# Weights times v by query halves: 1536 columns a unit for 2048, v's halves copied by its loads, and the filler's low parts on GpSimd

## The chip, the core and the metric

The kernel runs on one core of a Trainium2 chip. The metric is the device time of one execution in microseconds (us). A core has TensorE (PE, which multiplies matrices; PEld is its weight load), VectorE (DVE), ScalarE (ACT), GpSimd (POOL), and SyncE (SP), which here only issues DMAs. POOL issues some DMAs too; the queue of each of the two is in order.

## The reference

One block of a decoder, for 1024 tokens of 1024 channels: a modulated rmsnorm, one wide projection, two branches (sliding-window attention with sinks, and a linear recurrence), each gated and projected, merged by sigmoid gates, one output projection, a residual and a last rmsnorm. The change touches the attention alone:

```python
# 16 query heads in 4 groups (one k and v for 4 heads), head size 64, blocks of 128 queries
s = einsum('bnqkgd,bnskd->bnkgqs', qb, kb) / sqrt(64)   # 128 queries, 256 keys: own and last block
diff = qi + 128 - kj
band = (diff >= 0) & (diff < 128)                       # each query sees exactly 128 keys
m = maximum(max(s), sink)
p = exp(s - m);  denom = sum(p) + exp(sink - m)
o = einsum('bnkgqs,bnskd->bnqkgd', p / denom, vb)
```

A query q of block n sees the keys up to q of its own block and the keys behind q of the block before: for each of the 128 key positions exactly one of two. All is float32 in and out. Where the kernel multiplies in a shorter format it splits a number into a high and a low part (names in h and l: `phc`, `plc` for the weights, `wh`, `wl` for a projection's weights), and v's row holds both parts side by side, 64 columns each.

## The kernel before

The work is one long program, whose order on every engine is written out by hand up to the end of the attention. Behind that a list scheduler orders the tail.

Ahead of the attention come the modulation and the wide projection (`bk`, L709). Then follow 32 attention units, u = 0 to 31, eight query blocks n for each of the four groups, four heads in a unit. Between the steps of the units stand pieces of other matmuls, the filler: first the last of the projection, then the projection of the recurrent branch (`rp`, L173), which reads `yh` and `yl` (or, for the first two of eight rows, `hha` and `hla`) loaded from DRAM by SP, and weights `wh`, `wl`. Behind the attention come the projection of its output (`pmain`), the merge and the output projection.

A pass u of the loop does, on PE: the scores of unit u (`scores`, L1330, into the two banks of `s_ps`, which exist once), a piece of the filler (12 matmuls of 512 columns), the four transposes of unit u-2 (`transposed`, L1369, into `pt`), and the weights times v of unit u-3 (`values`, L1403, into `pv`). On ACT: the copy of the scores out of PSUM (L1339), the exponentials of unit u-1 (L1355), the high part `phc` of unit u-2 (L1374), half of the join of unit u-3 (L1412, L1413), a cast of filler weights (L105). On DVE: the scores of the last block where the mask asks for them (COPY_PREDICATED, L1345), the maximum (L1350), the low parts of the filler's weights (`rest`, L111), the division (L1362), the low part `plc` (L1380), the rest of the join (L1423, L1424), and the gating of finished pairs of units (L1538, L1548). On POOL: the sinks of unit u+1 (L1318), the masked copies `phm` and `plm` of unit u-2 (L1389), loads of v and some stores.

Since each key position stands for one key of two, only one transposed matrix of weights is kept for 128 positions, and the product is made as "all positions times the block before" plus "the masked positions times the difference of the two blocks". So a unit needs four matmuls: `phc` and `plc` with v of the block before, `phm` and `plm` with the difference. At n = 0 there is no block before, and two matmuls do. v of each group is prepared earlier (`v_prep`, L1154): `vs` is v in its two parts, `dv` the difference, and both are stored to `vd_d`, v shifted by one block. `load_v` (L1305) loads for two units at once, on POOL's queue, with two buffers.

The filler's weights go through `prep_r`: the cast is put on one list, the rest on another. The rests are issued on DVE in the next pass, ahead of the filler, and the casts on ACT at a pass's end. SP's queue takes the loads of keys, queries, gates, filler weights and of `yh`, `yl`.

In SBUF the tiles of attention are laid over tiles of the projection that are used no more. The first instruction that writes such a tile waits for the last that reads the old one. Among the old ones are the tiles from which `yh_d` and `yl_d` are stored, on POOL's queue, just ahead of the attention.

Of the kernel before, what the change touches and what calls it, by code (L numbers as in the profile page):

```python
# [12 lines left out]
F32 = mybir.dt.float32  # L13
# [5 lines left out]
ALU = mybir.AluOpType  # L19
# [31 lines left out]
BANKS = (0, 1, 2, 3), (4, 5, 6, 7)  # L51


@with_exitstack
def tile_hybrid_block(ctx, tc, x, pk, rows, posr, posi, c_row, w_ss, w_gate, w_main, w_v,
# [53 lines left out]
    def rest(dst, src, scale=1.0):  # L109
        if scale == 1.0:  # L110
            V.tensor_tensor(out=dst[1][:], in0=src, in1=f32(dst[0][:]), op=ALU.subtract)  # L111
# [18 lines left out]
    vd_d = [tc.dram_tile([P, 8, 2, P], F32, name=f"vd_d{g}") for g in range(NG)]  # L130
# [1023 lines left out]
    def v_prep(g):  # L1154
# [19 lines left out]
        def f3():  # L1174
# [3 lines left out]
            dma(vd_d[g][:, 1:8, 1, :], t["vs"][:, 0:7, :], G)  # L1178
            dma(vd_d[g][:, :, 0, :], t["dv"][:], G)
# [102 lines left out]
    def open_attn():  # L1282
# [9 lines left out]
        load_v(0)  # L1292

# [71 lines left out]
    def transposed(u):  # L1365
        px = U.pop(("s", u))[1]
        pt = psx.tile([P, 4, P], F32, tag="t", name="pt")
        for j in range(4):
            W["pe"] = T.transpose(pt[:, j, :], px[:, j, 0:P], ident[:])  # L1369
        U["t", u] = [pt]  # L1370

    def split_a(u):
        phc = at.tile([P, 4, P], F32R, tag="phc", name="phc")
        A.copy(phc[:], U["t", u][0][:])  # L1374
        U["t", u].append(phc)

    def split_d(u):
        pt, phc = U.pop(("t", u))
        plc = at.tile([P, 4, P], F32R, tag="plc", name="plc")
        V.tensor_tensor(out=plc[:], in0=pt[:], in1=f32(phc[:]), op=ALU.subtract)  # L1380
        U["m", u] = phc, plc

    def masks(u):
        phc, plc = U["m", u]
        ms = []
        if u % 8:
            for s_, tag in ((phc, "phm"), (plc, "plm")):
                d_ = W["yo"].tile([P, 4, P], F32R, tag=tag, name=tag)
                G.affine_select(out=d_[:], in_=f32(s_[:]), pattern=[[0, 4], [1, P]],  # L1389
                                compare_op=ALU.is_ge, fill=0.0, base=0,  # L1390
                                channel_multiplier=-1)
# [668 lines left out]
```

## Time and profile before

| | us |
|---|---|
| median of 3 runs | 907.04 (906.72 to 907.05) |
| the profiled execution | 907.17 |
| its span in the profile | 905.5 |
| PE busy | 895.4 (99%) |
| DVE busy | 717.1 (79%) |
| ACT busy | 567.4 (63%) |
| POOL busy | 124.7 (14%) |
| PE's granted clock | 0.999 |

All rows of the profile come from the profiled execution, whose time is its span and 1.67 us around it. The attention lies between 557.6 and 730.1 us of the span. A chain of waits is read from the end of the program back: at each step it goes to what released an instruction, or to the one before it on its engine. A row of a group of instructions gives line, engine, operation, what is written from what, the count, and then busy time and the mean of one in ns; behind the last bar stands the idle time of the engine ahead of it, and what ended it. A row of a stretch gives start and end, its length, the busy time of each engine with its count, PE's clock, the mean busy share of 16 DMA engines, and GB/s.

### The profile page before, as it was taken

What the parts mean: (1) busy time and instruction counts of PE and PEld (TensorE: products, weight loads), DVE (VectorE), ACT (ScalarE), POOL (GpSimd) and SP (SyncE); (2) the same over time, 40 slices, a digit from 0 to 9 for tenths busy, and PEclk for the clock granted to TensorE, in tenths of its full rate; (3) what the DMA queues carried; (4) which work ended last, traced back from release to release, by engine and by line L of the source; (5) the groups of instructions that cost most, each with busy time, mean ns of one, the idle gap of its engine ahead of it and who ended that gap; (6) DMA issues with size and microseconds to landing.
All of it is one profiled execution on the core that took longest, in us unless ns stands there. A gap on an engine that the chain in (4) does not pass through costs nothing.

```text
span 905.5 us, 12654 instructions
## 1 busy us (share of the span) xinstructions
PE 895.4 (99%) x4258; PEld 746.2 (82%) x4259; DVE 717.1 (79%) x1073; ACT 567.4 (63%) x1098; POOL 124.7 (14%) x216
## 2 busy tenths in 40 slices
PE   9999999999999999999999999999999999999997
PEld 6789888888888888888888888888888888888886
DVE  6987688988669875987788597999989846578855
ACT  7965554654566855786485884888888732115535
POOL 6520251200000000000000002343443300000000
PEclk9999999999999999999999999999999999999999
DMA  9829489772435353354446367996655289416604
GB/s 355 339 69 286 164 258 319 256 235 95 151 128 180 123 209 135 125 183 162 157 144 213 105 201 242 344 401 217 214 202 203 83 306 367 140 47 232 209 1 186
DMA packets 87349, 180.74 MB, mean 200 GB/s; under 512 B 8642, under 2 KB 29138, under 8 KB 87284
## 3 DMA queue, kind: packets, MB, share of 16 engines
q1 hardware_dynamic: 83200, 167.07, 52.5%
q0 software_dynamic: 3936, 12.59, 4.4%
q8 instruction: 34, 0.56, 0.3%
q14 instruction: 31, 0.25, 0.1%
q10 hardware_dynamic: 148, 0.27, 0.1%
HBM read 121.34 MB, written 58.95 MB: 199 GB/s over the span
## 4 chain that ended last, share of the span: by engine, by line
PE 52%; issue 42%; DVE 3%; ACT 2%; DMA 1%; POOL 0%; DVEq 0%; ACTq 0%; POOLq 0%
PE rp L173 14%; PE bk L709 10%; PE out L1863 6%; PE pmain L173 5%; PE s_ps L1330 3%; PE pv L1403 3%; PE pmain L485 2%; PE bk L485 2%; PE pt L1369 1%; DMA yl_d<-it 1%; PE pmain L1579 1%; PE pmain L1580 1%; PE pmain L1578 1%; ACT jk L1881 1%; PE bk L256 1%
## 5 line engine op out<-in xcount | busy, mean ns | idle before, releaser
L709 PE MATMUL bk<-nh,wh 128*128 128x512 f32 x368 | 143.4, 390 | 0.0
L709 PE MATMUL bk<-nl,wh 128*128 128x512 f32 x368 | 143.3, 389 | 0.0
L709 PE MATMUL bk<-nh,wl 128*128 128x512 f32 x368 | 98.4, 389 | 0.0
L111 DVE TENSOR_TENSOR wl<-r,wh 128x512 fp32r<-128x512 f32 x109 | 74.8, 692 | 23.3 <-ACT wh L105 23.2
L105 ACT CAST wh<-r 128x512 fp32r<-128x512 f32 x107 | 65.6, 618 | 32.1 <-PE rp L173 11.8
L709 PEld LDWEIGHTS bk<-nh,wl 128*128 128x128 f32 x368 | 69.1, 188 | 14.3
L709 PEld LDWEIGHTS bk<-nh,wh 128*128 128x128 f32 x368 | 69.2, 188 | 14.2
L709 PEld LDWEIGHTS bk<-nl,wh 128*128 128x128 f32 x368 | 69.1, 188 | 14.1
L709 PE MATMUL bk<-hh,wh 128*128 128x512 f32 x184 | 71.7, 390 | 0.0
L709 PE MATMUL bk<-hl,wh 128*128 128x512 f32 x184 | 71.6, 389 | 0.0
L111 DVE TENSOR_TENSOR wl<-ws,wh 128x512 fp32r<-128x512 f32 x76 | 52.1, 686 | 7.2 <-ACT wh L105 7.1
L62 POOL DMA_DIRECT2D yh_d<-av x1 | 0.6, 567 | 371.9 <-ACT av L1092 371.9
L1355 ACT ACTIVATE p<-p,small 128x129 f32<-128x129 f32 x128 | 50.0, 396 | 0.0
L709 PE MATMUL bk<-hh,wl 128*128 128x512 f32 x184 | 49.2, 389 | 0.0
L105 ACT CAST wh<-ws 128x512 fp32r<-128x512 f32 x76 | 46.0, 614 | 4.8 <-DVE ws L731 2.4
L709 PEld LDWEIGHTS bk<-hh,wl 128*128 128x128 f32 x184 | 34.6, 188 | 7.1
L709 PEld LDWEIGHTS bk<-hh,wh 128*128 128x128 f32 x184 | 34.6, 188 | 7.1
L709 PEld LDWEIGHTS bk<-hl,wh 128*128 128x128 f32 x184 | 34.6, 188 | 7.1
L1330 PEld LDWEIGHTS s_ps<-ks,qs 128*128 128x128 f32 x256 | 34.1, 189 | 4.4 <-DVE p L1345 2.0
L1330 PE MATMUL s_ps<-ks,qs 128*128 128x256 f32 (+1 forms) x256 | 35.6, 282 | 0.3 <-DVE p L1345 0.2
L709 PE MATMUL bk<-hha,wh 128*128 128x512 f32 x92 | 35.8, 390 | 0.0
L709 PE MATMUL bk<-hla,wh 128*128 128x512 f32 x92 | 35.8, 389 | 0.0
(378 smaller groups left out, 2293.1 us busy)
## 6 DMA issues: line engine op xcount, KB each, us to landing
r<-w_main SPq DMA_DIRECT2D x100, 256.0 KB, 4.2
wada<-w_ss SPq DMA_DIRECT2D x16, 512.0 KB, 9.0
qs<-q_d SPq DMA_DIRECT2D x16, 512.0 KB, 5.2
wo_d<-wr SPq DMA_DIRECT2D x28, 256.0 KB, 3.1
wo<-wo_d SPq DMA_DIRECT2D x14, 512.0 KB, 5.6
ks<-k_d SPq DMA_DIRECT2D x12, 384.0 KB, 4.3
xt<-x SPq DMA_DIRECT2D x8, 512.0 KB, 7.1
sma_d<-c SPq DMA_DIRECT2D x16, 256.0 KB, 4.4
```

Source lines behind the costliest of these rows:

```text
L105: A.copy(dst[0][:], src)
L111: V.tensor_tensor(out=dst[1][:], in0=src, in1=f32(dst[0][:]), op=ALU.subtract)
L173: mm = T.matmul(ps[hf], ww, xx[kc][hf], start=(kc == 0 and ww is w_h and xx is xh), stop=(kc == KC - 1 and xx is xl))
L256: T.matmul(bk[i % 2], zero[:, 0:P], zero, start=True, stop=True)
L485: T.matmul(starts[c][hf], ww[:, c0:c0 + P], xh[kc][hf], start=(kc == 0 and t_ == "h"), stop=(kc == KC - 1 and t_ == "l"))
L709: W["pe"] = T.matmul(ps, ww[:, kc * P:(kc + 1) * P], b[kc][i], start=(first and n == 0), stop=(n == 11), skip_group_check=not first)
L1330: W["pe"] = T.matmul(o, qs[:, j, qc], ks[:, kb:n % 2 + 2, b, :], start=(b == 0), stop=(b == 1))
L1355: A.activation(px[:, j, :], px[:, j, :], AF.Exp, bias=sm[:, 0, j:j + 1], accum_out=sm[:, 1, j:j + 1])
L1369: W["pe"] = T.transpose(pt[:, j, :], px[:, j, 0:P], ident[:])
L1403: W["pe"] = T.matmul(pv[:], b, m[:].rearrange("p j q -> p (j q)"), start=(i == 0), stop=(i == len(prods) - 1))
L1578: T.matmul(o, hh[kc][th][:, ts_], wh[:, cols], start=(kc == 0), stop=False)
L1863: T.matmul(o, a[k][x_][:, p * P:(p + 1) * P], b[k][y_][:, cols], start=(first and k == 0 and i == 0), stop=(k == 3 and i == 2), skip_group ...
```

## The change

`values` goes by halves of the 128 queries. For the first 64 queries (half l = 0) the key positions 64 to 127 always mean the block before; for the last 64 (l = 1) the positions 0 to 63 always mean the own block. So the mask decides in only 64 of the 128 positions of each half, and the masked high part and the masked low part of these 64 fit into one tile `pm` of 128 partitions. A half is three matmuls of 256 columns (`phc`, `plc`, `pm`), so a unit is six of 256 for four of 512. For that `pt`, `phc`, `plc` and `pv` are laid out by halves; `masks` makes four selects of 64 partitions x 256 for two of 128 x 512; the joins read another pattern. The units with n = 0 keep their two matmuls of 512.

The operand of v is then another one: for `phc` and `plc` at l = 1 the upper half of the partitions holds the own block and the lower the block before, and for `pm` the difference of one half of the positions stands twice. The stores no longer make that; the loads do. `v_prep` stores `vs` as it is and `dv` in two halves (three DMAs for two). `load_v` loads for each unit, two units ahead, with three buffers: two loads on SP's queue of 64 partitions each (64 KB each; the second reads each row twice) and one on POOL's (128 KB, which reads the rows twice); for n = 0 one load of 64 KB.

The rests of the filler's weights that are made during the attention go to GpSimd (`eng=G`), 18 of 128x512, and the two lists are both emptied at the end of a pass, behind the masks.

```diff
-    def rest(dst, src, scale=1.0):
+    def rest(dst, src, scale=1.0, eng=V):
         if scale == 1.0:
-            V.tensor_tensor(out=dst[1][:], in0=src, in1=f32(dst[0][:]), op=ALU.subtract)
+            eng.tensor_tensor(out=dst[1][:], in0=src, in1=f32(dst[0][:]), op=ALU.subtract)
...
-            dma(vd_d[g][:, 1:8, 1, :], t["vs"][:, 0:7, :], G)
-            dma(vd_d[g][:, :, 0, :], t["dv"][:], G)
+            dma(vs_d[g], t["vs"][:], G)
+            for l, half_ in enumerate((TOP, END)):
+                dma(dv_d[g][:, :, l, :], t["dv"][half_, :, :], G)
...
-    def load_v(m):
-        g, n0 = m // 4, (m % 4) * 2
-        vd = at.tile([P, 2, 2, P], F32R, tag="vd", name="vd", bufs=2)
-        if n0:
-            dma(vd[:], vd_d[g][:, n0:n0 + 2, :, :], G)
-        else:
-            dma(vd[:, 0, 0, :], vd_d[g][:, 0, 0, :], G)
-            dma(vd[:, 1, :, :], vd_d[g][:, 1, :, :], G)
-        U["v", m] = vd
+    def load_v(u):
+        g, n = u // 8, u % 8
+        vd = U["v", u] = at.tile([P, 2, 2, P], F32R, tag="vd", name="vd", bufs=3)
+        if not n:
+            dma(vd[:, 0, 0, :], vs_d[g][:, 0, :], G)
+            return
+        dma(vd[TOP, 0, :, :], vs_d[g][TOP, n - 1:n + 1, :])
+        dma(vd[END, 0, :, :], vs_d[g][END, n - 1, :].unsqueeze(1).to_broadcast([64, 2, P]))
+        dma(vd[:, 1, :, :], dv_d[g][:, n, :, :].unsqueeze(0).to_broadcast([2, 64, 2, P]), G)
...
-        pt = psx.tile([P, 4, P], F32, tag="t", name="pt")
+        pt = psx.tile([P, 2, 4, 64], F32, tag="t", name="pt")
         for j in range(4):
-            W["pe"] = T.transpose(pt[:, j, :], px[:, j, 0:P], ident[:])
-        U["t", u] = [pt]
+            W["pe"] = T.transpose(pt[:, :, j, :], px[:, j, 0:P], ident[:])
...
-            for s_, tag in ((phc, "phm"), (plc, "plm")):
-                d_ = W["yo"].tile([P, 4, P], F32R, tag=tag, name=tag)
-                G.affine_select(out=d_[:], in_=f32(s_[:]), pattern=[[0, 4], [1, P]],
-                                compare_op=ALU.is_ge, fill=0.0, base=0,
-                                channel_multiplier=-1)
-                ms.append(d_)
-        U["m", u] = [phc, plc], ms
+            pm = W["yo"].tile([P, HALF], F32R, tag="pm", name="pm")
+            lo, hi = slice(0, 256), slice(256, HALF)
+            for to, s_, from_, cols in ((TOP, phc, TOP, lo), (END, phc, END, hi),
+                                        (END, plc, TOP, lo), (TOP, plc, END, hi)):
+                G.affine_select(out=pm[to, cols], in_=f32(s_[from_, cols]),
+                                pattern=[[0, 4], [1, 64]], compare_op=ALU.is_ge, fill=0.0,
+                                base=0, channel_multiplier=-1)
+            U["m", u] = phc, plc, pm
...
-        for i, (b, m) in enumerate(prods):
-            W["pe"] = T.matmul(pv[:], b, m[:].rearrange("p j q -> p (j q)"),
-                               start=(i == 0), stop=(i == len(prods) - 1))
+        for l in range(2 if n else 1):
+            cols = slice(l * 256, l * 256 + 256) if n else slice(0, HALF)
+            for i, t_ in enumerate(m):
+                W["pe"] = T.matmul(pv[:, cols], vd[:, i // 2, l, :], t_[:, cols],
+                                   start=(i == 0), stop=(i == len(m) - 1))
...
-        if n % 2 == 0 and u // 2 + 1 < 16:
-            load_v(u // 2 + 1)
+        if u + 2 < 32:
+            load_v(u + 2)
...
-        do_later(later_d)
...
-        do_later(later_a)
+        do_later()
```

The order of PE's other matmuls is as it was. Three places of the order on other engines follow.

The first is ACT at the entry into the attention: the copy of the first unit's scores (`p<-s_ps`) and, three rows on, that of the second unit's. A name with DMASW in it is a DMA of POOL's queue, and the one named at the copies is the last store of `yl_d`. Before:

```order
L105 CAST wh<-ws 128x512 [waits PE_49,Activation_49]
L761 COPY bk_68<-bk_69 128x512 [waits PE_49]
L1339 COPY p<-s_ps 128x4x128 [waits PE_49,Activation_49]
L105 CAST wh<-r 128x512 [waits DMAHW7_49]
L758 COPY p_5378<-bk_71 128x512
L1339 COPY p<-s_ps 128x4x128 [waits DMASW0_49,PE_49]
```

And now:

```order
L106 CAST wh<-ws 128x512 [waits PE_49,Activation_49]
L763 COPY bk_68<-bk_69 128x512 [waits PE_49]
L1343 COPY p<-s_ps 128x4x128 [waits DMASW4_49,PE_49,Activation_49]
L106 CAST wh<-r 128x512 [waits DMAHW7_49]
L760 COPY p_5389<-bk_71 128x512
L1343 COPY p<-s_ps 128x4x128 [waits PE_49]
```

The rows are the same; the wait for the store has moved from the second unit's copy to the first's. POOL's first sink has it too.

The second is SP's queue in the passes in which the last `yh` and `yl` are loaded (the number behind a name tells the buffers apart; `yl_d5` is the sixth of eight). Before:

```order
L62 DMA yh_5841<-yh_d4_117 128x1024
L62 DMA yl_5842<-yl_d4_125 128x1024
L62 DMA yh_5913<-yh_d5_118 128x1024
L62 DMA yl_5914<-yl_d5_126 128x1024
L62 DMA r_5917<-w_rp 128x512
L62 DMA r_5919<-w_rp 128x512
L62 DMA r_5952<-ga_d0_93 128x512
L62 DMA ks_5964<-k_d_83 128x768
```

And now, with the v loads of units 6 and 7:

```order
L63 DMA yh_5874<-yh_d4_121 128x1024
L63 DMA yl_5875<-yl_d4_129 128x1024
L63 DMA vd_5892<-vs_d0_85 64x256
L63 DMA vd_5892<-vs_d0_85 64x2x128
L63 DMA yh_5951<-yh_d5_122 128x1024
L63 DMA yl_5952<-yl_d5_130 128x1024
L63 DMA r_5955<-w_rp 128x512
L63 DMA r_5957<-w_rp 128x512
L63 DMA vd_5973<-vs_d0_85 64x256
L63 DMA vd_5973<-vs_d0_85 64x2x128
L63 DMA r_5998<-ga_d0_97 128x512
L63 DMA ks_6010<-k_d_83 128x768
```

Each unit puts two loads between the others, behind the `yl` or the filler weights that were issued in the pass before.

The third is POOL in two passes around the start of the second group. Before:

```order
L1318 COPY p_5942<-pk_t_75 128x4
L1389 AFFINE_SELECT phm_5944<-phc_5933 128x512
L1389 AFFINE_SELECT plm_5946<-plc_5935 128x512
L62 DMA vd_6004<-vd_d1_86 128x128
L62 DMA vd_6004<-vd_d1_86 128x256
L1318 COPY p_6017<-pk_t_75 128x4
L1389 AFFINE_SELECT phm_6019<-phc_6007 128x512
L1389 AFFINE_SELECT plm_6021<-plc_6009 128x512
```

And now:

```order
L1322 COPY p_5986<-pk_t_75 128x4
L1394 AFFINE_SELECT pm_5988<-phc_5977 64x256 x2
L1394 AFFINE_SELECT pm_5988<-plc_5979 64x256 x2
L112 TENSOR_TENSOR wl_5995<-r_5484,wh_5994 128x512
L63 DMA vd_6051<-vs_d1_86 128x128
L1322 COPY p_6063<-pk_t_75 128x4
L1394 AFFINE_SELECT pm_6065<-phc_6053 64x256 x2
L1394 AFFINE_SELECT pm_6065<-plc_6055 64x256 x2
```

The four selects stand where the two stood, the rest is queued behind them and ahead of the next load and the next sink.

More of the change, by code (lines that the diff above doesn't have):

```diff
@@ L129, in tile_hybrid_block @@
     v_d = tc.dram_tile([P, 8, NG, 64], F32, name="v_d")
-    vd_d = [tc.dram_tile([P, 8, 2, P], F32, name=f"vd_d{g}") for g in range(NG)]
+    vs_d = [tc.dram_tile([P, 8, P], F32, name=f"vs_d{g}") for g in range(NG)]
+    dv_d = [tc.dram_tile([64, 8, 2, P], F32, name=f"dv_d{g}") for g in range(NG)]
     q_d = [tc.dram_tile([4, 512, 256], F32, name=f"q_d{g}") for g in range(NG)]
@@ L1366, in transposed @@
         px = U.pop(("s", u))[1]
-        pt = psx.tile([P, 4, P], F32, tag="t", name="pt")
+        pt = psx.tile([P, 2, 4, 64], F32, tag="t", name="pt")
         for j in range(4):
-            W["pe"] = T.transpose(pt[:, j, :], px[:, j, 0:P], ident[:])
-        U["t", u] = [pt]
+            W["pe"] = T.transpose(pt[:, :, j, :], px[:, j, 0:P], ident[:])
+        U["t", u] = [pt[:].rearrange("p l j q -> p (l j q)")]
     def split_a(u):
-        phc = at.tile([P, 4, P], F32R, tag="phc", name="phc")
-        A.copy(phc[:], U["t", u][0][:])
+        phc = at.tile([P, HALF], F32R, tag="phc", name="phc")
+        A.copy(phc[:], U["t", u][0])
         U["t", u].append(phc)
@@ L1378, in split_d @@
         pt, phc = U.pop(("t", u))
-        plc = at.tile([P, 4, P], F32R, tag="plc", name="plc")
-        V.tensor_tensor(out=plc[:], in0=pt[:], in1=f32(phc[:]), op=ALU.subtract)
+        plc = at.tile([P, HALF], F32R, tag="plc", name="plc")
+        V.tensor_tensor(out=plc[:], in0=pt, in1=f32(phc[:]), op=ALU.subtract)
         U["m", u] = phc, plc
@@ L1396, in values @@
         n = u % 8
-        vd = U["v", u // 2]
-        full, masked = U.pop(("m", u))
-        prods = [(vd[:, n % 2, 1 if n else 0, :], m) for m in full]
-        prods += [(vd[:, n % 2, 0, :], m) for m in masked]
+        vd = U.pop(("v", u))
+        m = U.pop(("m", u))
         pv = psx.tile([P, 4 * P], F32, tag="v", name="pv")
-        for i, (b, m) in enumerate(prods):
-            W["pe"] = T.matmul(pv[:], b, m[:].rearrange("p j q -> p (j q)"),
-                               start=(i == 0), stop=(i == len(prods) - 1))
@@ L1421, in join_d @@
             U["yq", u // 2] = W["yq"]
-        yo = W["yq"][:, :, (n % 2) * P:(n % 2 + 1) * P]
-        V.tensor_tensor(out=yo[0:64], in0=pvv[0:64, :, 0, :], in1=ob[0:64], op=ALU.add)
-        V.tensor_tensor(out=yo[64:128], in0=pvv[64:128, :, 1, :], in1=ob[64:128], op=ALU.add)
+        yo = W["yq"][:, :, (n % 2) * P:(n % 2 + 1) * P].rearrange("p a (l q) -> p l a q", l=2)
+        V.tensor_tensor(out=yo[0:64], in0=pvv[0:64, :, :, 0, :], in1=ob[0:64], op=ALU.add)
+        V.tensor_tensor(out=yo[64:128], in0=pvv[64:128, :, :, 1, :], in1=ob[64:128], op=ALU.add)
     ps_ctx = ExitStack()
@@ L1441, in prep_r @@
         later_a.append(f1)
-        later_d.append(lambda: rest(O[e, i], R[e][i]))
+        later_d.append(lambda: rest(O[e, i], R[e][i], eng=G if "att" in W else V))
         if "att" not in W:
```

11 lines of the change are left out of this document (6 added, 5 removed).

## The prediction

> **What bounds the kernel now.** I read the page first, then who waited for whom in the attention stretch, then the chain, then the stretches by time, and only then the entry into attention and the DMA queues.
>
> ```profile
> PE 895.4 (99%) x4258; PEld 746.2 (82%) x4259; DVE 717.1 (79%) x1073; ACT 567.4 (63%) x1098; POOL 124.7 (14%) x216
> PE s_ps L1330 <- DVE p L1345: 0.2, 1, 0.2
> 655.27 0.96 PE s_ps L1330 x8
> 656.23 2.75 PE rp L173 x12
> 658.98 0.44 PE pt L1369 x4
> 659.42 0.93 PE pv L1403 x4
> 664.48 0.92 PE pv L1403 x4
> 566.00:618.00 52.00, 51.91 (x290) 44.29 (x289) 48.62 (x89) 43.79 (x141) 19.46 (x37) 1.00 1.01 372
> 618.00:730.00 112.00, 112.00 (x608) 95.23 (x608) 99.08 (x184) 89.27 (x279) 42.00 (x74) 1.00 0.49 169
> 730.10:880.00 149.90, 149.90 (x662) 124.03 (x662) 101.84 (x133) 50.08 (x82) 0.00 (x0) 1.00 0.53 192
> ```
>
> PE is busy 99% of the span. The second row is the whole list of PE's waits between 557.6 and 731 us, the attention stretch: one, of 0.2 us. The chain there is one PE instruction behind the other: scores 0.96, filler 2.75, transposes 0.44, weights times v 0.93 (0.92 in the next pass), 5.1 us for a pass. So whatever PE no longer has to do is saved at once, as long as nothing else becomes late. The stretch rows (length, then busy time of PE, PEld, DVE, ACT, POOL; then PE's clock, DMA share, GB/s) show two regimes: until 618 the DMA engines are full (1.01), after it they are half idle (0.49), and PE is fully busy in both. After 730 there is no attention; the change only reorders a few casts and loads there, PE's order is the same, and I cost it at nothing (PE 149.90 of 149.90 covers it; its cover gone, it would be some tenths).
>
> **Weights times v.** In 28 of the 32 units four matmuls of 512 columns become six of 256. No pv of 256 columns is in the trace; the nearest row is s_ps, eight matmuls of mostly 256 columns with a weight load each in 0.95 to 0.96 us, 0.119 us each. Six take 0.71 us where four took 0.925: 0.2125 us a unit, 28 x 0.2125 = 6.0 us. The upper bound, no gain at all, I keep as a rival. The clock is 1.00 in these rows, so it is the same price. Seven of the units (1 to 7) lie before 618 us and 21 behind it: 1.5 and 4.5 us.
>
> **The entry.** The tiles of the attention lie elsewhere in SBUF, since yo is 2 KB a partition smaller. By the order, the first copy of scores (ACT) and the first sink (POOL) now wait for the store of yl_d; before, that fell to the second unit's. The trace around it, the chain's row first:
>
> ```profile
> 554.00 8.30 DMA yl_d<-it
> 558.94 0.59 ACT L1339 COPY p<-s_ps 128x512 f32<-128x512 f32 x1 [2.38 <-PE s_ps L1330]
> 559.60 0.64 POOL L1348 TENSOR_SCALAR_AFFINE_SELECT p<-p 128x512 f32<-128x512 f32 x1 [2.25 <-ACT p L1339]
> 561.51 1.11 PE L1330 MATMUL s_ps<-ks,qs 128*128 128x256 f32 x8
> 562.42 0.69 DVE L1350 TENSOR_REDUCE small<-p 128x4 f32<-128x516 f32 x1 [5.12 <-DMA yl_d<-it]
> 563.03 0.68 DVE L111 TENSOR_TENSOR wl<-ws,wh 128x512 fp32r<-128x512 f32 x1
> 563.63 0.69 DVE L829 SCALAR_TENSOR_TENSOR c<-c 128x512 f32<-128x512 f32 x1
> 564.23 0.68 DVE L731 TENSOR_TENSOR ws<-ws,r 128x512 f32<-128x512 f32 x1
> 564.83 0.73 DVE L1345 COPY_PREDICATED p<-mgt,s_ps 128x512 f32<-128x512 uint32 x1
> 565.62 0.61 PE L1330 MATMUL s_ps<-ks,qs 128*128 128x256 f32 x3 [0.24 <-DVE p L1345]
> ```
>
> The store lands at 562.30. DVE's reduction waited for it already, with 5.12 us idle, and PE's third scores waited 0.24 at the end of that. Now the copy starts at 562.35 and ends at 562.94; PE's second scores, which need the s_ps banks it reads, start at 562.95 and not 561.51; POOL's select ends at 563.6; DVE reduces until 564.3 and goes through the next three, 0.6 us from start to start, to the COPY_PREDICATED at 566.1 to 566.85. The third scores start at 566.9, against 565.62: **+1.3 us**. Queued behind the waiting copy on ACT are a cast, another copy and the exponentials of unit 0; DVE waits for them, and PE through DVE. If the store lands as before this cost is nearly certain; its bounds are 0 (the store 1.4 us earlier) and 1.5 (PE's second scores late in full).
>
> **The loads of v.** A unit took half of a 256 KB load (POOL queue, 2 KB runs); now it takes 256 KB: 128 KB on the POOL queue and two of 64 KB on SP's, of 64 partitions each, one in 512-byte runs. What a byte costs, by the queue's rows of 566:618 and of 70:80 (the k_d stores, 512-byte runs):
>
> ```profile
> q1 hardware_dynamic: 6530, 16.99, 87.4%
> q1 hardware_dynamic: 5066, 2.51, 85.9%
> vd<-vd_d POOLq DMA_DIRECT2D x4, 256.0 KB, 6.4
> yl<-yl_d SPq DMA_DIRECT2D x6, 512.0 KB, 9.9
> L62 SPq DMA_DIRECT2D yl<-yl_d x6: 319/404/773, 582.0 to 606.6; - x6
> L173 PE MATMUL rp<-yl,wh x20: 389/390/395, 596.5 to 618.3; 128*128 128x512 f32 x20
> 593.08 0.50 SPq L62 DMA_DIRECT2D yl<-yl_d  x1
> 593.62 1.55 SPq L62 DMA_DIRECT2D yh<-yh_d  x1
> 596.28 2.04 SPq L62 DMA_DIRECT2D r<-w_rp  x2
> 603.75 0.47 PE L1403 MATMUL pv<-phc,vd 128*128 128x512 f32 x1
> ```
>
> Engine time per byte: 0.874 x 16 x 52 us / 16.99 MB = 0.0428 ns for the large runs, 0.859 x 16 x 10 us / 2.51 MB = 0.0547 ns for 512 bytes. A unit's 256 KB cost 64 KB x 0.0547 + 192 KB x 0.0428, over 16 engines 0.75 us, against 0.35: 0.40 us more. Behind 618 the share of 0.49 hides it (0.40 of 4.85 us is 8 points). Before 618 nothing is free, and the loads of units 2 to 7 stand ahead of the last yl load on SP: 6 x 0.40 = 2.4 us. Seen by turns, SP issued 12 loads from the row at 593.08 to the last yl at 606.6, 13.5 us in 11 steps, 1.2 us each, and the four v loads among them (units 6 and 7) would cost 4 x 1.2 = 4.8. These are two views of one queue, so I take neither their sum (7.2, the upper bound) nor zero (the lower one) but the middle of the two, 3.6. The last yl load, issued at 606.6 and landing 9.9 later, at 616.5, would land at 620.1. PE's last matmul that reads yl comes at 618.3, with the change at 618.3 + 1.3 - 1.5 = 618.1: **+2.0 us** of waiting, with 0 to 5.6 for the bounds. [...]
>
> **GpSimd and VectorE.** 18 rests of the filler's weights, 128x512, go from DVE to POOL, and two selects of 128x512 become four of 64x256.
>
> ```profile
> L111 DVE TENSOR_TENSOR wl<-r,wh 128x512 fp32r<-128x512 f32 x19 | 13.2, 693 | 0.0
> L1389 POOL TENSOR_SCALAR_AFFINE_SELECT plm<-plc 128x512 fp32r<-128x512 f32 x28 | 17.7, 632 | 15.0 <-DVE plc L1380 14.4 <-PE s_ps L1330 0.6
> L62 POOL DMA_DIRECT2D vd<-vd_d x18 | 9.9, 554 | 2.3 <-PE pv L1403 2.0 <-issue 0.3
> L224 POOL CAST wh<-r 128x512 fp32r<-128x512 f32 x2 | 1.2, 612 | 0.5 <-DMA r<-w_main 0.4
> L1362 DVE TENSOR_TENSOR p<-p,small x32: 691/693/1094, 567.1 to 719.7; 128x512 f32<-128x512 f32 x32
> L1389 POOL TENSOR_SCALAR_AFFINE_SELECT phm<-phc x28: 629/649/1127, 575.3 to 726.5; 128x512 fp32r<-128x512 f32 x28
> 624.35 0.74 DVE L1345 COPY_PREDICATED p<-mgt,s_ps 128x512 f32<-128x512 uint32 x1
> 628.81 0.74 DVE L1345 COPY_PREDICATED p<-mgt,s_ps 128x512 f32<-128x512 uint32 x1
> ```
>
> A DVE pass without a rest takes 4.46 us from one COPY_PREDICATED to the next, with one 0.6 more, 5.07. PE's new pass is 5.06 - 0.21 = 4.85. So DVE, with its rests, would be just too slow for it, and without them it has 0.39 us spare. On POOL a pass is a sink (0.3), a DMA issue (0.55), four selects and, in 18 passes, a rest. A select of 64x256 costs between half a 128x512 one (0.32, half the columns) and all of it (0.63); a rest, with two inputs, between the cast of that size (0.61) and two of them (1.22). That is 2.7 to 4.6 us in 4.85: it fits, at both ends. The rests are queued behind the selects of a pass and in front of the next sink, which DVE's reduction needs a pass later, so I cost the move at 0, hidden by PE's pass; with that cover gone each rest costs what POOL is late, at most 1.2. v's stores are three a group on POOL's queue for two, while POOL is idle (14% busy in all): nothing.
>
> **The sum**, on the profiled execution (907.17: span 905.5 and 1.67 around it): 907.17 - 6.0 + 1.3 + 2.0 = 904.5. The median of the runs is 0.13 lower, so 904.3 against 907.04. 0.2%, 1.8 us, is what a measurement of this kernel can tell from no change: faster is below 905.2, slower above 908.9.
>
> **The rivals.**
>
> *The DMA queue takes it.* Late y loads end at the bound of 7.2, a wait of 5.6: 907.17 - 6.0 + 1.3 + 5.6 = 908.1, or 907.9 against the median, the end of my forecast's own band. The rival that ends slower is another one: the v loads themselves are late. SP works in order, and the loads of units 2, 6, 7 and 9 stand behind hla, yl and yh loads that land late. By the rows, unit 6's two loads are issued after 593.6, at 1.2 us each, so the second at 596.0, and with 9.9 us to land they are there at 605.9. PE reads v of unit 6 at 603.75 + 1.3 - 5 x 0.2125 = 604.0: 1.9 late, and PE stands, since pv is next in its order. Five units (2, 5, 6, 7, 9) at 1.9 make 9.5: 907.17 - 6.0 + 1.3 + 9.5 = 912.0, 911.8 against the median. It decides from 6.5 us of lateness on. For it: the landing time of yl and the full queue. Against it: vd landed in 6.4 us in that stretch, which would be 602.4, in time; and a wait for v gives the y loads time, so the two do not add.
>
> *GpSimd and VectorE lock each other.* In the last rows POOL's select and DVE's multiplication, 0.65 and 0.69 at the median, each reach 1.1 at times: they lose 0.4 us to something, and both read SBUF. If a rest of up to 1.1 us stops DVE for its whole length, a pass in which it meets one of DVE's two operations with two SBUF inputs (1.4 of 4.46 us, so about half of the 18) costs 1.1 - 0.39 = 0.7 us: 9 x 0.7 = 6.3, half of it won back in the next pass without a rest, 3.1: 904.5 + 3.1 = 907.6, 907.5 against the median. Against it: the median of 32 is 693, so few are stretched. [...]
>
> *The queue gives way.* The y loads start no later than before, the bytes fit in, and only the entry costs: 907.17 - 6.0 + 1.3 = 902.5, 902.3 against the median (901.0 if the entry is free too). For it: PE waited for no DMA at all before, though the share was 1.01.
>
> *Six small ones cost what four large ones did.* Then nothing is gained; PE comes to the last yl matmul at 618.3 + 1.3 = 619.6 and waits 0.5: 907.17 + 1.3 + 0.5 = 909.0, 908.8 against the median. Against it: the s_ps rows.
>
> **How the numbers follow.** The forecast, some of the gain given back at the entry and in the full queue, has 0.50 and a band of its own from 902.7 (entry late, queue nearly free) to 907.9 (the queue's upper bound); 0.36 of it lies below 905.2. The queue gives way: 0.14, all faster. The lock: 0.15, 0.12 of it within 0.2%, 0.03 slower. Late v loads: 0.15, of it 0.13 slower. No gain from the smaller matmuls: 0.06, of it 0.04 within. Faster: 0.36 + 0.14 = 0.50; within 0.2%: 0.14 + 0.12 + 0.02 + 0.04 = 0.32; slower: 0.13 + 0.03 + 0.02 = 0.18. The range of 901.5 to 909.0 holds the forecast's band, the queue that gives way and the lock's price; most of the late loads and a corner below are left out, 0.19.
>
> **What would show it.** In the profile after, pv is six rows in 0.71 us in the chain and a pass behind 618 us is 4.85: the term of 6.0 is right; 0.8 or more, and it is wrong. The first scores copy on ACT ends its idle time on the store of yl_d and PE's second scores start near 563: the entry is right. PE's list of waits, one row of 0.2 now, shows rp waiting for yl or hla (the forecast, about 2 us in all), pv waiting for vd (late v loads), s_ps or pv waiting for DVE or POOL with DVE rows near 1.1 us (the lock), or nothing (the queue gave way). The forecast is wrong if PE's waits between 566 and 618 sum to over 5 us or if passes behind 618, where the queue is half idle, are longer than 4.9.

## The result and the profile after

The changed kernel takes 918.16 us, the median of 4 runs (917.23 to 920.48), against 906.92 for the kernel before beside it: 1.0128 times as long, with a 95% interval of 1.0107 to 1.0149. It is 11.2 us slower where 2.7 us faster was forecast, and above the range. The profiled execution took 920.48, its span 918.5; it is the longest of the four, so its rows hold 13.0 us of loss where the medians are 11.2 apart.

From the page of the kernel after: the busy row of PE, and the DMA packets of the whole run (before: 87349 packets, of them 8642 under 512 B).

```profile
PE 898.2 (98%) x4315; PEld 749.4 (82%) x4315; DVE 710.4 (77%) x1055; ACT 567.8 (62%) x1098; POOL 171.8 (19%) x306
DMA packets 100215, 184.78 MB, mean 201 GB/s; under 512 B 16067, under 2 KB 41939, under 8 KB 100149
```

From the stretches of after: the first two from 566 us on, then two short ones in which PE's clock was granted at half. The columns are length, busy time of PE, PEld, DVE, ACT, POOL, PE's clock, DMA share, GB/s.

```profile
566.00:618.00 52.00, 45.57 (x249) 39.48 (x248) 39.72 (x73) 38.10 (x122) 29.86 (x53) 0.90 1.01 301
618.00:680.00 62.00, 58.60 (x348) 49.68 (x347) 51.26 (x91) 47.69 (x150) 37.86 (x67) 1.00 0.92 247
...
587.10:593.90 6.80, 5.22 (x19) 4.81 (x20) 2.67 (x5) 3.80 (x12) 2.98 (x6) 0.50 0.90 264
614.40:617.80 3.40, 3.40 (x12) 2.89 (x12) 3.03 (x5) 3.15 (x13) 2.40 (x5) 0.50 1.02 292
```

In 566:618 the DMA engines are as full as before, 1.01, but they move 301 GB/s where they moved 372, and PE stands for 6.43 of 52 us. The loss is there and just behind it. These are PE's waits of over 1 us in the attention stretch of after (total, times, longest); before, the whole list was one row of 0.2:

```profile
PE pv L1407 <- DMA vd<-vs_d: 4.7, 2, 3.9
PE pv L1407 <- DVE p L1366: 2.5, 1, 2.5
PE rp L175 <- DMA yl<-yl_d: 1.4, 2, 0.8
PE rp L175 <- DMA yh<-yh_d: 1.1, 1, 1.1
```

The chain of after between 573 and 617 us, and then an undisturbed pass (start, length, what):

```profile
573.00 6.97 DMA r<-ga_d
579.99 8.56 DMA vd<-vs_d
588.68 1.62 PE pv L1407 x6
590.30 1.71 PE s_ps L1334 x8
592.01 3.73 PE rp L175 x12
...
596.49 0.45 POOL smr_d L63
597.05 7.99 DMA smr_d<-c
605.13 0.90 DVE al L1552
606.03 1.04 DVE yq L1542
...
613.18 0.95 PE pv L1407 x6
614.13 1.38 PE s_ps L1334 x8
615.51 3.88 PE rp L175 x12
...
653.90 0.71 PE pv L1407 x6
654.61 0.95 PE s_ps L1334 x8
655.57 2.75 PE rp L175 x12
658.32 0.44 PE pt L1373 x4
658.75 0.71 PE pv L1407 x6
```

The chain, which was one PE instruction behind the other, now goes through DMAs: a load of v lands at 588.6 and PE stands 3.9 us for it; a store lands at 605.0, DVE is late with what follows, and PE stands 2.5 us at 613. Behind each of the two the same instructions take longer: pv, scores and filler 7.06 and 6.21 us, against 4.41 in the last pass. That is 2.65 and 1.80 us more, in the two stretches with the clock at 0.50.

Measured from the start of one unit's scores to the next, before and after, seven passes carry the loss: units 5 (+4.58), 6 (+1.55), 9 (+2.30), 10 (+1.24), 12 (+3.57), 15 (+0.79) and 26 (+0.50), 14.5 us together. The second unit's scores are 1.36 late, of which the first unit's were 0.63 late already. The other passes give 3.0 back, mostly 0.2 each. So the last unit's scores start 12.9 late, and the end is 13.0 late.

The DMA queues of after in 566:618 (queue: packets, MB, share; loads with count, KB and time to landing):

```profile
DMA packets 8604, 15.64 MB, mean 301 GB/s; under 512 B 2261, under 2 KB 3913, under 8 KB 8598
...
q0 software_dynamic: 1984, 1.92, 13.1%
...
vd<-dv_d POOLq DMA_DIRECT2D x7, 128.0 KB, 9.9
vd<-vs_d SPq DMA_DIRECT2D x12, 64.0 KB, 8.5
```

The load of 128 KB on POOL's queue takes 9.9 us to land, where the 256 KB load of before took 6.4.

### The profile page after: what moved, and what is told of

Its sections match the earlier page's. It is cut to its first block, busy times and chain, and to the rows that moved or that the text cites. A ratio compares the mean times of both kernels' runs of the same rounds, so it can differ in the third digit from the quotient of the medians.

```text
span 918.5 us, 12978 instructions
## 1 busy us (share of the span) xinstructions
PE 898.2 (98%) x4315; PEld 749.4 (82%) x4315; DVE 710.4 (77%) x1055; ACT 567.8 (62%) x1098; POOL 171.8 (19%) x306
## 4 chain that ended last, share of the span: by engine, by line
issue 47%; PE 33%; DMA 10%; DVE 4%; POOL 3%; ACT 3%; SPq 0%; POOLq 0%; DVEq 0%; ACTq 0%
PE rp L175 11%; PE out L1866 4%; PE pmain L175 4%; DMA vd<-vs_d 3%; PE bk L487 3%; PE pmain L487 2%; PE s_ps L1334 2%; PE pv L1407 2%; DMA wo<-wo_d 2%; PE bk L711 1%; DMA vd<-dv_d 1%; DMA yl_d<-it 1%; DMA smr_d<-c 1%; PE pmain L1583 1%; PE pmain L1584 1%
## 5 line engine op out<-in xcount | busy, mean ns | idle before, releaser
L106 ACT CAST wh<-r 128x512 fp32r<-128x512 f32 x107 | 65.5, 617 | 26.8 <-PE rp L175 11.9
L112 DVE TENSOR_TENSOR wl<-r,wh 128x512 fp32r<-128x512 f32 x91 | 61.9, 688 | 21.9 <-ACT wh L106 21.9
L1378 ACT CAST phc<-pt 128x512 fp32r<-128x512 f32 x32 | 18.8, 586 | 35.2 <-PE pv L1407 23.7
L1384 DVE TENSOR_TENSOR plc<-pt,phc 128x512 fp32r<-128x512 f32 x32 | 22.0, 688 | 19.2 <-ACT phc L1378 18.7
```

Source lines behind the costliest of these rows:

```text
L106: A.copy(dst[0][:], src)
L112: eng.tensor_tensor(out=dst[1][:], in0=src, in1=f32(dst[0][:]), op=ALU.subtract)
L1378: A.copy(phc[:], U["t", u][0])
L1384: V.tensor_tensor(out=plc[:], in0=pt, in1=f32(phc[:]), op=ALU.subtract)
```

## The experiments

All kernels compute the whole of what the reference does. The theories at the start, with the letters of the expectations: SP's in-order queue makes v's loads late (A); they crowd the queue by their form, 64 partitions, rows read twice, three DMAs for a unit (B); twice the bytes are too much (C); GpSimd's rests stop VectorE (D).

### Which part of the change costs the time

`rest_dve` gives the filler's rests back to DVE.

```diff
-        later_d.append(lambda: rest(O[e, i], R[e][i], eng=G if "att" in W else V))
+        later_d.append(lambda: rest(O[e, i], R[e][i]))
```

> The 18 rests go back to DVE, in the order of the kernel before; all else as in the changed kernel. A, B, C: no gain, 917 to 921 (DVE a little late in passes with a rest). D: 908 to 912.

It took 916.94 (ratio 1.0103, 1.0086 to 1.0120). Its wait list still has v first:

```profile
PE pv L1407 <- DMA vd<-vs_d: 7.2, 2, 4.9
```

That is 1.2 below the change, with intervals that overlap. So the loss isn't between GpSimd and VectorE.

`v_act` issues SP's two loads from ACT's queue instead.

```diff
-        dma(vd[TOP, 0, :, :], vs_d[g][TOP, n - 1:n + 1, :])
+        dma(vd[TOP, 0, :, :], vs_d[g][TOP, n - 1:n + 1, :], A)
```

(and the second load likewise)

> The two 64-partition loads are issued from ACT's queue and not SP's, so they stand behind no y load; form and bytes as in the changed kernel. A: PE's waits for vd go, 904 to 907 (some tenths for ACT's issues). B: the engines stay slow, GB/s about 300 to 320, 914 or more, with waits for yl instead of vd. C: as B. D: 916 or more.

It took 921.02 (1.0154, 1.0139 to 1.0169) at 299 GB/s in 566:618. PE waits for v for only 0.4 us there, and the loads land in 7.0 us for 8.5, but ACT, which works in order, was held by them, and PE waits for what ACT and DVE then make late. From ACT's part of its wait list:

```profile
ACT phc L1378 <- DMA vd<-vs_d: 9.0, 3, 5.3
```

`v_full` makes SP's two loads one of 128 partitions, from a DRAM tile that four stores fill; POOL's load of dv stays as it is.

```diff
-            dma(vs_d[g], t["vs"][:], G)
+            dma(vx_d[g][:, 1:8, 0, :], t["vs"][:, 0:7, :], G)
+            dma(vx_d[g][:, 0, 0, :], t["vs"][:, 0, :], G)
+            dma(vx_d[g][TOP, 1:8, 1, :], t["vs"][TOP, 1:8, :], G)
+            dma(vx_d[g][END, 1:8, 1, :], t["vs"][END, 0:7, :], G)
...
-        dma(vd[TOP, 0, :, :], vs_d[g][TOP, n - 1:n + 1, :])
-        dma(vd[END, 0, :, :], vs_d[g][END, n - 1, :].unsqueeze(1).to_broadcast([64, 2, P]))
+        dma(vd[:, 0, :, :], vx_d[g][:, n, :, :])
```

> The two SP loads of 64 partitions become one of 128 partitions x 1 KB (128 KB) on SP; its copies are made by the stores; the POOL load with its row read twice stays. Same bytes, same queues, one SP DMA a unit for two. A: half the turns on SP are gone, so about half of the 11 us: 911 to 913. B: the 64-partition loads were what slowed the engines, so most of it goes: 905 to 908, over 350 GB/s in the stretch. C and D: 916 or more.

It took 916.70 (1.0108, 1.0083 to 1.0132), 320 GB/s in 566:618. That is the time that theories C and D gave it, but not for their reason: in its profile the first scores are already 5.1 us late, behind standstills of up to 1.9 us in the projection, near the added stores. From the first scores to the last it loses 2.7 us more, where after loses 12.3; PE still waits 3.6 us for v.

`v_wide` goes all the way: the stores make every copy, eight a group, and a unit's v is one 256 KB load on POOL's queue.

```diff
-        dma(vd[:, 1, :, :], dv_d[g][:, n, :, :].unsqueeze(0).to_broadcast([2, 64, 2, P]), G)
+        dma(vd[:], vx_d[g][:, n, :, :, :], G)
```

(SP's two loads are gone, too; the eight stores are not shown)

> All of v's copies are made by the stores; a unit takes one load of 256 KB, 128 partitions x 2 KB, on POOL's queue, and nothing on SP's. Bytes as in the changed kernel. Theory A (the v loads are late because they stand in SP's in-order queue behind the y loads): PE's waits for vd go, about 904 to 906 us. Theory B (64 partitions and short runs make the full DMA engines slower: 301 GB/s for 372): the same, and the stretch 566:618 is back near 370 GB/s. Theory C (twice the bytes are what is too much): still 912 or more. Theory D (the rests on GpSimd and VectorE's operations block each other): still 916 or more.

It took 919.17 (1.0136, 1.0114 to 1.0157), and yet the attention in it was right. Its list of PE's waits before the attention begins with

```profile
PE bk L712 <- DVE wl L114: 7.3, 1, 7.3
```

Between 124 and 199 us, where the extra stores are, loads of weights came late (DVE stood 13.2 us for `wr<-w_gate`), and with them the low parts that PE waits for here. At the first scores this kernel is 15.4 us late, at the last 11.9: in the attention it gained 3.5, with no wait for v or y. So the stores were a poor way to make the copies, and the loads of v were what cost the attention its time.

### The same loads, with the copies made elsewhere

`wide_copies` keeps the stores of the change, makes the copies by 20 DMAs from DRAM to DRAM on SP's queue, one in about 13 us, long before the attention, and loads as `v_wide` does.

```diff
+    def v_copies(g):
+        x, vs, dv = vx_d[g], vs_d[g], dv_d[g]
+        for i, (to, from_) in enumerate(((x[:, 1:8, 0, 0, :], vs[:, 0:7, :]),
+                                         (x[TOP, 1:8, 0, 1, :], vs[TOP, 1:8, :]),
+                                         (x[END, 1:8, 0, 1, :], vs[END, 0:7, :]),
+                                         (x[TOP, :, 1, :, :], dv[:]), (x[END, :, 1, :, :], dv[:]))):
+            at_slot(44 + 4 * (5 * g + i), ("S", 0, 0, lambda to=to, from_=from_: dma(to, from_, nc.sync)))
```

> v's stores as in the changed kernel; twenty DRAM-to-DRAM copies on SP, one every four slots (11 us) of the projection, lay v out as the units need it; a unit is one load of 256 KB, 128 partitions x 2 KB, on POOL's queue. Theory B (the form of the loads, 64 partitions, rows read twice and short runs, slows the full DMA engines): the attention gains 3.5 us as with the wide load before, and the projection loses nothing: 903 to 905. Theory C (the doubled bytes): waits for yl or hla from 566 to 618, 908 or more. Theory A (SP's queue alone): 903 to 905 too.

It took 903.09 (0.9958, 0.9943 to 0.9973): faster than both kernels. Its row of 566:618, and the one wait of PE in the attention:

```profile
566.00:618.00 52.00, 51.54 (x307) 44.66 (x306) 47.53 (x85) 45.29 (x145) 33.83 (x62) 1.00 1.02 390
```

```profile
PE s_ps L1341 <- DVE p L1356: 0.3, 1, 0.3
```

The same 256 KB a unit go into SBUF as in the change, and the queue moves 390 GB/s at the share at which it moved 301. So the bytes fit; it is the form of the loads.

`wide_sp` puts that load on SP's queue (`nc.sync` for `G`).

> As the one with the copies, but the load of 256 KB is issued on SP's queue, behind the y loads. A: units 2, 6, 7 and 9 are late again, PE waits for vd, 908 to 914. B: the form is good, so the queue matters little, 903 to 906, near 380 GB/s from 566 to 618.

903.96 (0.9968, 0.9957 to 0.9979), 382 GB/s: the in-order queue of SP is no reason either. `wide_dve` is `wide_copies` with the rests on DVE.

> As the one with the copies, with the 18 rests back on DVE. Theory D in its small form (POOL's longer work costs DVE some tenths a pass): 0 to 2 us less. Against it, by DVE's 5.07 us for a pass with a rest and PE's 4.85: 0.2 us more for up to 18 passes, 1 to 4 us more.

904.17 (0.9972, 0.9960 to 0.9984), 1.1 us above `wide_copies`, with intervals that overlap: if the rests matter, POOL is the better place. `dv_wide` takes the double reading out of POOL's load alone, by stores that write dv twice; SP's loads stay as in the change.

```diff
-                dma(dv_d[g][:, :, l, :], t["dv"][half_, :, :], G)
+                for to in (TOP, END):
+                    dma(dx_d[g][to, :, l, :], t["dv"][half_, :, :], G)
...
-        dma(vd[:, 1, :, :], dv_d[g][:, n, :, :].unsqueeze(0).to_broadcast([2, 64, 2, P]), G)
+        dma(vd[:, 1, :, :], dx_d[g][:, n, :, :], G)
```

> Only the POOL load changes: the differences of v are stored twice (four stores of 256 KB for two), and a unit's POOL load is 128 partitions x 1 KB without a row read twice; the two SP loads of 64 partitions stay. B with the SP loads as what slows: no better, 914 to 919. B with the POOL load that reads rows twice as what slows (its packets under 512 B): 906 to 910 and over 350 GB/s. A: 914 to 919.

909.26 (1.0028, 1.0017 to 1.0040), 341 GB/s, though its extra stores cost it time before the attention, as in `v_wide` (its first scores are 8.4 us late in its profile, which at 914.33 is the longest of seven runs). Most of the loss is gone, and SP's two loads are still there: this points at POOL's load.

### Which property of the loads

Three kernels with the copies of `wide_copies`, measured together. `form_wide` loads 128 KB on SP and 128 KB on POOL, both of 128 partitions. `form_twice` differs from it in one line: POOL's load reads 64 rows twice, as in the change. `form_halves` has POOL's load in two of 64 partitions.

```diff
-        dma(vd[:, 1, :, :], vx_d[g][:, n, 1, :, :], G)
+        dma(vd[:, 1, :, :], dv_d[g][:, n, :, :].unsqueeze(0).to_broadcast([2, 64, 2, P]), G)
```

> The kernel with the copies, its load cut in two of 128 KB and 1 KB runs: v of the two blocks on SP, the differences on POOL, each 128 partitions and no row read twice. It is the base for the next two. If runs of 1 KB instead of 2 KB cost little: 903 to 905, 370 GB/s or more from 566 to 618. If short runs are what slows the engines: 907 or more, under 350 GB/s.

> As the base, but the differences are read as in the changed kernel: 64 rows of 1 KB, each read twice, in one DMA of POOL's queue to 128 partitions. Same bytes into SBUF, same queues, same count. If this form is the larger part of the loss: 908 to 914, 310 to 340 GB/s. If the 64 partitions of the SP loads were: 903 to 906.

> As the base, but the differences come in two POOL loads of 64 partitions, 64 KB each, from rows that stand twice in DRAM, so none is read twice. If 64 partitions a DMA are what slows: 907 to 912, under 350 GB/s. If reading a row twice is: 903 to 906 (one more POOL issue of 0.6 a pass).

`form_wide` 904.11 (0.9968, 0.9957 to 0.9978), `form_twice` 911.63 (1.0050, 1.0034 to 1.0065), `form_halves` 904.23 (0.9969, 0.9958 to 0.9981). Of `form_wide` the row of 566:618, then POOL's load there, then the same load in 690:725, where the queue is half idle:

```profile
566.00:618.00 52.00, 51.57 (x306) 44.49 (x306) 47.84 (x86) 45.00 (x143) 31.22 (x61) 1.00 1.02 376
```

```profile
vd<-vx_d POOLq DMA_DIRECT2D x8, 128.0 KB, 5.7
```

```profile
vd<-vx_d POOLq DMA_DIRECT2D x6, 128.0 KB, 2.4
```

And the same three of `form_twice`, with PE's longest wait ahead of them:

```profile
PE pv L1415 <- DMA vd<-vx_d: 3.5, 2, 3.3
```

```profile
566.00:618.00 52.00, 47.17 (x269) 41.02 (x269) 41.35 (x74) 38.19 (x121) 30.60 (x54) 0.93 1.01 326
```

```profile
vd<-dv_d POOLq DMA_DIRECT2D x7, 128.0 KB, 9.4
```

```profile
vd<-dv_d POOLq DMA_DIRECT2D x7, 128.0 KB, 5.3
```

One line costs 7.5 us and 50 GB/s, and PE's clock falls to 0.93 in the mean of the stretch. Where the queue is half idle the load lands 2.9 us later. And the load that PE waits for longest is another one, SP's. Its rows of 566:618, in `form_wide` and in `form_twice`:

```profile
vd<-vx_d SPq DMA_DIRECT2D x9, 128.0 KB, 7.0
```

```profile
vd<-vx_d SPq DMA_DIRECT2D x7, 128.0 KB, 9.1
```

The load beside the slow one lands 2.1 us later (9.1 for 7.0).

`no_twice` is the change with no row read twice: its queues, its sizes, its 64 partitions, the sources from the copies. `sp_twice` lets SP's second load read its rows twice again, the copy being an inner dimension there ([64, 2, P]).

```diff
-        dma(vd[END, 0, :, :], vs_d[g][END, n - 1, :].unsqueeze(1).to_broadcast([64, 2, P]))
-        dma(vd[:, 1, :, :], dv_d[g][:, n, :, :].unsqueeze(0).to_broadcast([2, 64, 2, P]), G)
+        dma(vd[END, 0, :, :], vx_d[g][END, n, 0, :, :])
+        dma(vd[:, 1, :, :], vx_d[g][:, n, 1, :, :], G)
```

> The changed kernel's loads in queue, count, size and partitions (two of 64 partitions on SP, one of 128 KB on POOL), but every row is read once, from rows that the paced copies made. If reading rows twice is the whole loss: 903 to 905 and 360 GB/s or more from 566 to 618. If 64 partitions on SP or two more turns a unit there cost too: 907 or more.

> As no_twice, with the second SP load reading each of its 64 rows of 512 bytes twice, as in the changed kernel. If a double read on SP's queue costs as on POOL's (7.5 us there for twice the bytes): 906 to 910. If only POOL's queue pays for it: within 1 us of no_twice.

905.81 (0.9992, 0.9983 to 1.0001) and 906.08 (0.9991, 0.9981 to 1.0000), 10 runs each. Reading rows twice costs nothing that can be seen in SP's load (0.3 us, with intervals that overlap). In POOL's it costs the change 12.1 us (918.16 to 906.08): it is the load whose outermost dimension is the two copies. `no_twice` lies between its two expectations, at 351 GB/s.

Beside one load of 128 partitions on SP the same line cost 7.5 us, beside two of 64 it costs 12.1. So some 4.6 us come only when both are there; why, no run here shows.

### Why that load is slow

`dv_sp` is the change with that load on SP's queue, and nothing else. It was to tell POOL's queue from the load itself.

```diff
-        dma(vd[:, 1, :, :], dv_d[g][:, n, :, :].unsqueeze(0).to_broadcast([2, 64, 2, P]), G)
+        dma(vd[:, 1, :, :], dv_d[g][:, n, :, :].unsqueeze(0).to_broadcast([2, 64, 2, P]))
```

> The changed kernel with one word changed: the load that reads 64 rows twice is issued on SP's queue and not on POOL's. If POOL's queue is what makes the double read dear: 905 to 908, near 350 GB/s from 566 to 618, and few packets under 512 B. If reading rows twice costs on both: 914 or more.

936.84 (1.0332, 1.0315 to 1.0349). So it is not POOL's queue; on SP's the load costs far more. Its longest wait in the attention, then its DMA rows of 640:660 (40 slices of 0.5 us: share in tenths, GB/s), then its row of 706.0:707.2:

```profile
PE pv L1407 <- DMA vd<-dv_d: 20.1, 12, 3.3
```

```profile
DMA  9524211163499113379998773411111198979999
GB/s 346 189 56 123 71 47 47 45 162 100 145 373 334 55 45 121 129 309 416 418 385 336 274 233 77 118 55 43 45 45 45 45 248 260 213 285 361 367 381 293
```

```profile
706.00:707.20 1.20, 1.20 (x10) 0.99 (x8) 0.19 (x1) 1.20 (x6) 1.00 (x1) 1.00 0.13 47
```

The slices fall again and again to a share of 0.1 and 43 to 47 GB/s and stay there for up to 2.5 us. In the last row the share is 0.13: 0.13 x 16 = 2.1 engines. And 45 GB/s, at the 390 / 16 = 24.4 GB/s that one engine moves in `wide_copies`, is 1.8 engines. Counted from its packet records between 690 and 725 us, exactly two packets are in flight 21% of the time and one or none for less than 1%; in `form_wide` none is for 36% and exactly two for 2%. With the load on POOL's queue, in after, exactly two are for 9%, in the kernel before for 1%. So the load runs on two of the 16 DMA engines; that each takes half of its 128 KB is an estimate. 128 KB at 45 GB/s are 2.9 us, where at 390 GB/s they are 0.3; that is about the 2.9 us by which the load lands later in `form_twice`.

The records of the semaphores, in which a DMA leaves several updates up to its landing, agree with it and show one thing more. Each of the 28 loads of this form left 3 updates in `dv_sp`, where nearly all other DMAs of SP left 16: the load issued at 703.12 has one at 704.05 and then two, at 709.56 and 713.50. Of the other DMAs of SP in 690:725 (the 19 that can be matched with their updates) the first 14 updates come within 0.8 us in the median, and the last 3.9 us behind the 14th; in `form_wide` it comes 0.2 us behind. So the loads beside it stand 3.9 us for their last two updates. That these two come from the two busy engines is an inference; the records do not name the engine of an update. With the load on POOL's queue the effect is smaller: in 618:690 the last update comes 0.9 us behind the 14th in `form_twice` and 1.2 in after, for 0.1 in `form_wide` and 0.3 in the kernel before.

The times to landing of v's loads in 690:725 agree with two engines for this load: with 64 or 128 rows outermost, and no [2, 64] beside them, those of 64 and 128 KB land in 2.3 to 3.2 us in the median (one for an n = 0 took 3.3, in 680:730 of `form_wide`), also where an inner dimension repeats (`sp_twice`, 2.8), and [2, 64] takes 5.3 (`form_twice`). With this load the kernel takes 936.84 on SP's queue and 918.16 on POOL's; why SP's is the worse place for it, no run here shows, and the traces do not number the engines.

`dv_two` is the change with that load cut into two, each of 64 partitions that reads the 64 rows once, with no copies made; its tile pool for `p` is also moved, as in the next experiment.

```diff
-        dma(vd[:, 1, :, :], dv_d[g][:, n, :, :].unsqueeze(0).to_broadcast([2, 64, 2, P]), G)
+        dma(vd[TOP, 1, :, :], dv_d[g][:, n, :, :], G)
+        dma(vd[END, 1, :, :], dv_d[g][:, n, :, :], G)
```

> The changed kernel with that load as two of 64 partitions on POOL's queue, each reading the 64 rows once, and the p tiles of the attention ahead of the yo tiles; no copies. If the double read in one DMA of POOL is the cause: 903.5 to 906 (no_twice less the entry's 1.6, and one more POOL issue). If the same rows read by two DMAs cost as much: 912 or more.

907.51 (1.0007, 0.9998 to 1.0016), 10 runs, above the 906 expected at most: 335 GB/s, and 3.7 us of waiting for SP's loads of v are left. So without copies the change is no faster than the kernel before, even with this load mended and the entry freed. The form of that load makes up most of the loss (12.1 of it in `sp_twice`); what the four loads of 64 partitions still cost here, some 3 us over `no_twice` less its entry, was not taken apart.

### The entry

`entry_free` and, at another time, `entry_again` are `wide_copies` with the pool of the `p` tiles opened ahead of that of `yo`, so that the first unit's `p` no longer lies where the store of `yl_d` reads. `copies_again` is `wide_copies` once more, beside `entry_again`.

```diff
-        W["yo"] = pool(at_ctx, "yo", side="right")
...
+        W["yo"] = pool(at_ctx, "yo", side="right")
```

(the line moves down two lines, behind the pool of `p`)

> The kernel with the copies, the p tiles of the attention placed ahead of the yo tiles, so that the first copy of scores waits for no store of yl_d. If the entry costs what the forecast put there: the second scores come 1 us or more earlier against the first than in the changed kernel (4.40 apart there), 902 to 902.5 us. If the store's landing holds DVE's reduction all the same: within 0.3 of the kernel with the copies.

> The kernel with the copies once more, as the base of the next: 902.5 to 904.

> The one with the p tiles moved, on the same chip as its base. If the wait for the store costs the forecast's 1.3: 1.0 us or more below the base. If the reduction's wait holds PE all the same: within 0.4.

`entry_free` 902.28 (0.9951, 0.9934 to 0.9967). `copies_again` 903.93 (0.9968, 0.9956 to 0.9979) and `entry_again` 902.31 (0.9952, 0.9939 to 0.9964), 1.6 us apart; `wide_copies` and `entry_free`, measured at different times, are 0.8 apart. In the attention, the wait over 1 us of `copies_again`, and all of `entry_again`:

```profile
PE s_ps L1341 <- ACT p L1350: 1.3, 1, 1.3
```

```profile
PE s_ps L1341 <- DVE p L1356: 0.4, 1, 0.4
```

The wait for ACT's copy of scores goes with the move. What it costs differs from profile to profile: from the first scores to the second it is 3.67 us in the kernel before and in the kernels with the move, 4.40 in after, and in kernels with the copies and without the move from 3.73 (`wide_copies`) to 5.17 (`wide_sp`). So against after the move wins 0.73, less than the 1 us that was expected of `entry_free`. At 902.3 this is the fastest of all kernels, 4.6 us below the kernel before.

## Why the prediction was wrong, point by point

**Weights times v: right.** Six matmuls take 0.71 us in the chain and a pass 653.90 to 658.75, 4.85, both as forecast. The gain of 0.2 a pass shows in the passes that wait for nothing.

**The entry: the mechanism right, the nearness of its size luck.** In after, ACT's first copy of scores and PE's second scores:

```profile
562.23 0.58 ACT L1343 COPY p<-s_ps 128x512 f32<-128x512 f32 x1 [5.60 <-DMA yl_d<-it]
562.87 1.22 PE L1334 MATMUL s_ps<-ks,qs 128*128 128x256 f32 x8 [0.57 <-ACT p L1343]
```

The copy waits for the store, and the scores start at 562.87 for the 562.95 forecast. 1.3 was forecast, for the third scores; the second are 1.36 late in the profile and the third 1.14, but 0.63 of that was there at the first scores, and 0.73 came from the first to the second. In the other profiles with this entry that is between 0.06 and 1.50, and the medians of kernels that differ by it are 0.8 and 1.6 apart. Where in this range one execution falls, the prediction could not say.

**The loads of v: the step that failed.** It priced them by "what a byte costs" and by turns on SP's queue, +2.0 with 5.6 as the bound. The term measured 14 to 15: 918.16, against 903.09 to 903.96 where a unit's v is one load of 256 KB (`wide_copies`, `copies_again`, `wide_sp`). The bytes did fit: 390 GB/s with the same 256 KB a unit and no wait for a load, so in that form the term is about 0. What the step left out is how many engines a load is spread over. It took every load at a sixteenth of its bytes for each engine, and the load of [2, 64] rows ran on two (`dv_sp`, a share of 0.13); on POOL's queue its form alone is 12.1 us (`sp_twice`). This form stood in the diff, and none of the rows of before that the prediction shows has it. The reads of yl did come late, 1.4 us for yl and 1.1 for yh, 2.5 against the 2.0 forecast, but behind 6.4 us of other waits, and for another reason, so that the two are near is luck.

**The second price that was missing** is the clock. The prediction costed a late load at its lateness. With a standstill of 3.9 us the clock was granted at 0.50 for 6.8 us, from 587.1, 1.6 before its end; with one of 2.5 for 3.4 us, from 614.4, 1.2 behind its end. That cost 2.65 and 1.80 more, 4.45 of the 12.9 us. It does not follow each time: behind a standstill of 3.0 us in `v_full` and one of 2.7 in `dv_sp` the clock stayed full. What decides it, no run here shows.

**Full and half-empty.** The prediction let the share of 0.49 behind 618 hide the loads. It was 0.92 in 618:680 after, for 0.57 before, and PE waited for y and v there for 3.2 us (0.7 of it for v). So the cover that the prediction named was thinner than its row said.

**64 partitions.** `form_halves`, with two loads of 64 partitions on POOL for one of 128, is 0.1 above `form_wide`: no cost can be seen. `no_twice`, with SP's loads in halves, is 1.7 above `form_wide`, measured at another time, and this holds the further issue on SP too. Beside the slow load the halves cost more: 918.16 in the change, 911.63 in `form_twice`, whose load on SP is one of 128 partitions. So on POOL's queue the measurement gives them no price; on SP's, what the 64 partitions cost and what the second load costs is not told apart.

**The rivals.** PE stood for v first of all, as the rival of late loads had it at 911.8 and 0.15, but not for that rival's reason: `wide_sp` puts the whole load on SP's in-order queue and stays at 903.96. Its size was too small for the two reasons above. (It names four units whose loads stand behind late ones, and counts five; four would have made 909.9.) The lock did not show in the time: with the rests on POOL or on DVE it is the same within 1.3 us, in the change and in `wide_copies`. That a rest stops DVE for its whole length, and only where an operation has two SBUF inputs, was a supposition; no run shows it. Single rows of DVE near 1.1 us stand in both kernels. But a rest on POOL took more than the bound of 1.22, by the row of after's groups between 557 and 740 us:

```profile
L112 POOL TENSOR_TENSOR wl<-r,wh 128x512 fp32r<-128x512 f32 x16 | 23.2, 1449 | 9.3 <-ACT wh L106 7.7 <-POOL pm L1394 0.6
```

At 1.45 it is twice DVE's 0.69, and still hidden. "The queue gives way", 902.3 with 0.14 and 901.0 with the entry free, comes nearest to what the change does once all its loads of v are replaced by one wide load from copies: 903.1 to 904.0 with the entry late, 902.3 with it free. With POOL's load alone mended it is 906.08, 0.9 below the kernel before.

**What would show it wrong** was met: PE's waits in 566:618 are 6.4 us, over the 5, and some passes behind 618 are longer than 4.9, that of unit 12 with 8.65 the longest.

## What to carry to other kernels

When a load's source repeats rows, look where the repeating dimension stands: outermost, it left two of 16 DMA engines at work (`dv_sp`, a share of 0.13) and cost 12.1 us on POOL's queue; inside, behind 64 rows, it cost nothing that could be seen (0.3 us). The slow load also delayed the one beside it (9.1 us for 7.0 in `form_twice`), and a full DMA share did not show it (1.01 at 326 GB/s, 1.02 at 376): read GB/s beside the share, and look in a half-idle stretch for slices at a small share that last. And price a standstill of PE with what the clock can add to it: two of 6.4 us together cost 4.45 more here.

## What the runs showed of the hardware

- At a share of 1.01 to 1.02 the DMA engines moved 301, 326, 376 or 390 GB/s, by the form of the loads of v.
- A load of [2, 64] rows on SP's queue left two DMA engines at work, 43 to 47 GB/s, 47 at a share of 0.13 (`dv_sp`). With it on SP's queue the kernel took 936.84 us, on POOL's 918.16.
- With standstills of PE of 2.5 and 3.9 us came 3.4 and 6.8 us at half the clock; with others, of 2.7 and 3.0 us, none (`dv_sp`, `v_full`).
- Eight stores of v a group in the projection, where the kernel before has two, put the first scores 15.4 us later. With 20 copies from DRAM to DRAM, one in about 13 us, they came between 0.6 us earlier and 1.1 later in the profiles, and in the change without the copies 0.6 later.
